# Reordering the weight splits of the pair jobs in a hybrid encoder layer, and two small products from high and low parts

## The chip, the cores and the metric

The kernel runs on one core of a Trainium2 chip. The time is that of one execution on the device, in microseconds (us). Shown are the median and the spread of several runs, and one execution taken by the hardware profiler. The engines are TensorE (PE, with its weight loads PEld), VectorE (DVE), ScalarE (ACT), GpSimd (POOL) and SyncE (SP, which issues DMAs). Each takes its instructions in the order in which the program lists them.

## The reference

One layer of a streaming encoder for 512 tokens of width 1024, all in float32: a SwiGLU feed-forward network (FFN, hidden width 2816) with half a residual, a mixer (a gated linear recurrence beside sliding-window attention), and a second FFN. Each is wrapped in RMS norms. What bears on the change is cut to this:

```python
def swiglu(x, w1, w3, w2):
    return (jax.nn.silu(x @ w1) * (x @ w3)) @ w2

f = swiglu(rms_norm(h, ffn1_pre_g), ffn1_w1, ffn1_w3, ffn1_w2)
h = h + 0.5 * rms_norm(f, ffn1_post_g)
...                      # mixer; attention adds bias = table[buckets]
f = swiglu(rms_norm(h, ffn2_pre_g), ffn2_w1, ffn2_w3, ffn2_w2)
h = h + 0.5 * rms_norm(f, ffn2_post_g)
```

## The kernel before, in words

Products must be accurate to float32, and the fast float32r format keeps fewer bits. So every operand is split: `split2` lets ScalarE copy it into float32r (the high part, `hi`) and VectorE subtract that copy from the original (the low part, `lo`). Each product is then three: high by high, low weight by high, high weight by low.

The up-projections w1 and w3 of both FFNs run mostly as *pair jobs* (class `Pairs`). A job takes two blocks of 128 hidden units of one of the two weights and computes their outputs for all 512 tokens as a 2x2 block product, by a Strassen scheme of the Winograd form: seven block products instead of eight, paid with sums of blocks. The blocks of the weight are a11, a12 (first raw tile, `ra`) and a21, a22 (second, `rb`). The weight sums are S1 = a21 + a22, S2 = S1 - a11 (one tile, `S12`), S3 = a11 - a21, S4 = a12 - S2 (one tile, `S34`). The activations' sums T1 to T4 are made once. A block product (`mm_s`, L464) is 12 products of 256 columns: 4 slices of the contraction, each the three of high and low parts.

The first FFN has 18 jobs (w1 and w3 in turn, job 0 to 17), the second 20. In `run` a job's products stand in this order: a11, S1, then a22 of the job before (it adds to a bank that the job before still holds, `last`, L591), S2, a12, S4, S3. Between them the next job is prepared, by `prep(m, i)`: i = 0 makes S1 and S2 (on GpSimd from job 2 on, and two jobs ahead), i = 1 splits `ra`, i = 2 makes S3 and S4 on VectorE and splits `S12`, i = 3 splits `S34`, i = 4 splits a22. ScalarE also copies four banks of each job to SBUF: q1 (L550), q5 (L553), u (L559) and v (L579). The bank of v is the one to which the next job's a22 product adds, so that product waits for the copy of v. In the first FFN the input norm's factor per token (`Rb`) is multiplied in behind the product: after an odd job's a22 product ScalarE copies the bank (L594), VectorE multiplies the w1 output with `Rb` (L595), and ScalarE takes the silu of it (L596), which `run` issues behind the next split of S34.

In the last job, a12 comes last, and `tail` (`w2_ahead`) splits two hidden units and two weights for the down-projection ahead of time.

Two small products are made in full float32, which TensorE takes in several passes: the row factor (`factor`, L714: ones times four diagonal matrices, so that each token's factor stands in all partitions), and the bias rows (`bias_rows`, L730: the relative-bias table times a one-hot matrix, 16 by 384), which stands between a11 and S1 of job 3.

Tiles of up to 4 KB per partition come from a pool of 42 slots; a tile that is given back is taken by a later one, which then waits for the last reader. The tiles `gap` and `gap2` hold nothing: they only shift the addresses of what follows.

Of the kernel before, what the change touches and what calls it, by code (L numbers as in the profile page):

```python
# [51 lines left out]
def hybrid_layer(ctx: ExitStack, tc: tile.TileContext, a: dict, out: bass.AP):  # L52
# [10 lines left out]
    def slot(shape, dt=F32, name="s"):  # L63
        uid[0] += 1
        return sb.tile(shape, dt, tag="slot", name=f"{name}_{uid[0]}")
# [5 lines left out]
    def small(w, name="m", bufs=4):  # L71
        uid[0] += 1
        return sm.tile([P, w], F32, tag=f"sm{w}", name=f"{name}_{uid[0]}", bufs={1: 11, 4: 12}.get(w, bufs))
# [11 lines left out]

    veps = cp.tile([P, NT], F32, name="veps")

    cp.tile([P, 172], F32, name="gap")
    sm.tile([P, 256], F32, name="gap2", bufs=1)
    uT = cp.tile([P, 2, KT, SEQ], F32R, name="uT")  # L90


# [383 lines left out]
    class Pairs:  # L476
# [14 lines left out]
        def prep(self, m, i, eng=None):  # L491
            if m >= len(self.jobs) or (m, i) in self.ready:
                return
            self.ready.add((m, i))
            k = self.k0 + 2 * m
            if i == 0:
                if k not in loaded or k + 1 not in loaded:
                    self.raws(m)
                s12, s34 = slot([P, 2 * QH], name="S12"), slot([P, 2 * QH], name="S34")
                self.w[m] = {"r": (raws.pop(k), raws.pop(k + 1)), "s": (s12, s34)}  # L500
            W = self.w[m]
            (ra, rb), (s12, s34) = W["r"], W["s"]
            a11, a12, a21, a22 = ra[:, :QH], ra[:, QH:], rb[:, :QH], rb[:, QH:]

            def both(src, w=2 * QH):
                hi = slot([P, w], F32R, name="whi")
                lo = slot([P, w], F32R, name="wlo")
                split2(hi, lo, src)
                return hi, lo

            def halves(p, a, b):
                W[a] = p[0][:, :QH], p[1][:, :QH]
                W[b] = p[0][:, QH:], p[1][:, QH:]

            if i == 0:
                e = eng or pool
                e.tensor_tensor(out=s12[:, :QH], in0=a21, in1=a22, op=ALU.add)
                e.tensor_tensor(out=s12[:, QH:], in0=s12[:, :QH], in1=a11, op=ALU.subtract)
            elif i == 1:
                halves(both(ra), "a11", "a12")  # L520
            elif i == 2:
                dve.tensor_tensor(out=s34[:, QH:], in0=a12, in1=s12[:, QH:], op=ALU.subtract)
                dve.tensor_tensor(out=s34[:, :QH], in0=a11, in1=a21, op=ALU.subtract)  # L523
                halves(both(s12), "s1", "s2")
            elif i == 3:
                halves(both(s34), "s3", "s4")
            elif i == 4:
                t = slot([P, 2, QH], F32R, name="w22")
                split2(t[:, 0, :], t[:, 1, :], a22)
                W["a22"] = t[:, 0, :], t[:, 1, :]  # L530
            if all((m, x) in self.ready for x in range(5)):
                del W["r"], W["s"]

        def run(self, tail, hooks={}):
            X = self.X
            assert st["get"] == st["split"] == self.k0, (st, self.k0)
            st["get"] = st["split"] = self.k0 + 2 * len(self.jobs)
            last = silu = lambda: None
            for n, (nm, f) in enumerate(self.jobs):
                W = self.w.pop(n)  # L540
                first = nm == self.na
                tmp = slot([P, 4, 256], name="ct")
                q1, q5, u, v = (tmp[:, i, :] for i in range(4))
                c = slot([P, 2, SEQ], name="cc")
                if first:
                    self.c1[f] = c
                bu, bx, bc = (bank("c")[:, :256] for _ in range(3))
                at = lambda i: [f() for f in hooks.get((n, i), ())]
                mm_s(W["a11"], X["b11"], bu)
                act.activation(q1, bu, AF.Copy)  # L550
                at(1)
                mm_s(W["s1"], X["t1"], bx)
                act.activation(q5, bx, AF.Copy)  # L553
                at(2)
                silu = last() or silu
                self.prep(n + 1, 1)
                mm_s(W["s2"], X["t2"], bu, True)
                del W["s1"], W["s2"]
                act.activation(u, bu, AF.Copy)  # L559
                at(3)  # L560
                if n == len(self.jobs) - 1:
                    tail()
                self.prep(n + 1, 2)

                def c11():
                    mm_s(W["a12"], X["b21"], bc)
                    del W["a11"], W["a12"]
                    dve.tensor_tensor(out=c[:, 0, :256], in0=bc, in1=q1, op=ALU.add)

                if n < len(self.jobs) - 1:  # L570
                    c11()
                mm_s(W["s4"], X["b22"], bx, True)
                dve.tensor_tensor(out=c[:, 0, 256:], in0=bx, in1=u, op=ALU.add)
                self.prep(n + 1, 3)
                silu()
                silu = lambda: None
                mm_s(W["s3"], X["t3"], bu, True)
                del W["s3"], W["s4"]
                act.activation(v, bu, AF.Copy)  # L579
                dve.tensor_tensor(out=c[:, 1, 256:], in0=v, in1=q5, op=ALU.add)  # L580
                if n == len(self.jobs) - 1:
                    c11()
                if not first:
                    c1 = self.c1[f]
                    dve.tensor_tensor(out=c1[:, 0, :], in0=c1[:, 0, :], in1=c[:, 0, :], op=ALU.mult)
                    dve.tensor_tensor(out=c1[:, 1, 256:], in0=c1[:, 1, 256:], in1=c[:, 1, 256:], op=ALU.mult)
                self.prep(n + 1, 4)
                self.prep(n + 2, 0)
                self.raws(n + 3)

                def last(W=W, bu=bu, c=c, f=f, first=first):  # L591
                    mm_s(W.pop("a22"), X["t4"], bu, True)
                    if first and self.R is not None:
                        act.activation(c[:, 1, :256], bu, AF.Copy)  # L594
                        dve.tensor_tensor(out=c, in0=c, in1=self.R, op=ALU.mult)  # L595
                        return lambda: act.activation(c, c, AF.Silu)  # L596
                    if first:
                        act.activation(c[:, 1, :256], bu, AF.Silu)
                        act.activation(c[:, 0, :], c[:, 0, :], AF.Silu)
                        act.activation(c[:, 1, 256:], c[:, 1, 256:], AF.Silu)  # L600
                    else:
                        c1 = self.c1.pop(f)
                        dve.tensor_tensor(out=c1[:, 1, :256], in0=bu, in1=c1[:, 1, :256], op=ALU.mult)
                        self.hid.f += [c1[:, 0, :], c1[:, 1, :]]

            last()
# [47 lines left out]
    dma_one(pairs_a.k0)  # L654
    dma_one(pairs_a.k0 + 1)
    make_identity(nc, ident)
    ones = slot([P, P], name="ones")
    pool.memset(ones, 1.0)
    ps = [bank("f") for _ in range(NS)]

    def split_first(u, kp):
# [34 lines left out]
    def t_split(n):  # L696
        X1[f"t{n + 1}"] = to_slots(tg[n])

    dgs = slot([P, NT, P], name="dgs")

    s4 = small(NT, "s4")

    def squares():
        for t in range(NT):
# [3 lines left out]
    def root():  # L708
        r = rstd4(s4)
        act.activation(tiny, tiny, AF.Silu)  # L710
        for t in range(NT):
            dve.tensor_scalar(out=dgs[:, t, :], in0=ident, scalar1=r[:, t : t + 1], scalar2=NEWT, op0=ALU.mult, op1=ALU.mult)

    def factor():  # L714
        psr = bank("r")
        for t in range(NT):
            pe.matmul(psr[:, t * P : (t + 1) * P], ones, dgs[:, t, :], start=True, stop=True)
        for i in range(2):
            act.activation(Rb[:, i, :], psr, AF.Copy)

# [2 lines left out]
    oh, erow = [], []  # L723

    def bias_in():
        oh.append(slot([N_BUCKETS, NREL + 1 + N_HEADS], name="oh"))
        pool.dma_start(out=oh[0][:, : NREL + 1], in_=a["onehot"])
        pool.dma_start(out=oh[0][:, NREL + 1 :], in_=a["rel_bias"])

    def bias_rows():  # L730
        pse = bank("e")
        t = oh.pop()
        pe.matmul(pse[:N_HEADS, : NREL + 1], t[:, NREL + 1 :], t[:, : NREL + 1], start=True, stop=True)
        erow.append(slot([N_HEADS, NREL + 1], name="erow"))
        act.activation(erow[0], pse[:N_HEADS, : NREL + 1], AF.Copy)

# [88 lines left out]
        late[4 + i, 1] = [lambda i=i: bias_spread(i)]  # L825

    def w2_ahead():
        hid.to(1)
        split_to(st["split"] + 1)
        hid.to(2)  # L830
        split_to(st["split"] + 1)

    pairs_a.run(w2_ahead, late)
# [460 lines left out]
```

## Time and profile before

| What | Value |
|---|---|
| Median of 3 runs | 1136.23 us (1135.98 to 1136.77) |
| The profiled execution: its time, and its span | 1137.54 us, 1135.5 us |
| TensorE busy | 1125.4 us (99%) |
| VectorE busy | 790.0 us (70%) |
| ScalarE busy | 597.8 us (53%) |
| GpSimd busy | 241.1 us (21%) |
| Pair jobs of the first FFN | from 50.9 to about 236 us |
| Pair jobs of the second FFN | from 806.4 to about 1008 us |
| Granted TensorE clock | 0.998 |

The profile gives for each instruction the engine, its line in the kernel, the tiles that it writes and reads, its start and its duration. A record of a product overlaps the next, so TensorE's busy time says little about its pace; the distance between the starts of products says it. Idle time before an instruction is given with what ended it, and a line such as L194 is that of a helper (`split2`): the tiles tell who called it.

### The profile page before, as it was taken

The numbers are of one execution on the slowest core, as the hardware profiler recorded it, in microseconds if no ns is written. First come the engines' busy times: TensorE is split into PE (matmuls) and PEld (weight loads), VectorE is DVE, ScalarE is ACT, GpSimd is POOL, SyncE is SP. The second block draws the span as 40 slices with busy tenths as digits, with TensorE's granted clock in tenths as the row PEclk, the third lists the DMA queues.
The fourth block names the chain that finished last, engine by engine and source line by source line (L and its number), as shares of the span: only waits on it lengthen the run. The fifth ranks groups of instructions, "written<-read, shape, count | busy, mean of one in ns | idle before, by whom it ended". The sixth has DMA issues, their size and how long they took to land.

```text
span 1135.5 us, 17456 instructions
## 1 busy us (share of the span) xinstructions
PE 1125.4 (99%) x6835; PEld 1006.0 (89%) x6835; DVE 790.0 (70%) x1252; ACT 597.8 (53%) x1060; POOL 241.1 (21%) x203
## 2 busy tenths in 40 slices
PE   9999999999999999999999999999999999999997
PEld 7899999988888987888888888889999999998886
DVE  5898989885336747695678865767787777885313
ACT  7755655574324349944656653356555555573211
POOL 0035444200000000001555641000533233300000
PEclk9999999999999999999999999999999999999999
DMA  9235563264313411234122333531333332265101
GB/s 324 96 103 137 122 150 113 75 222 151 110 56 130 149 57 56 75 94 148 56 80 89 93 102 103 187 109 39 111 101 99 100 112 94 74 195 176 38 19 56
DMA packets 37139, 124.95 MB, mean 110 GB/s; under 512 B 4529, under 2 KB 6449, under 8 KB 37057
## 3 DMA queue, kind: packets, MB, share of 16 engines
q1 hardware_dynamic: 34272, 115.15, 30.8%
q0 software_dynamic: 2640, 8.43, 3.8%
q8 instruction: 53, 0.87, 0.3%
q10 hardware_dynamic: 144, 0.26, 0.1%
q14 instruction: 30, 0.24, 0.1%
HBM read 116.50 MB, written 7.33 MB: 109 GB/s over the span
## 4 chain that ended last, share of the span: by engine, by line
PE 91%; DVE 5%; ACT 3%; issue 1%; DMA 0%; SPq 0%; DVEq 0%; ACTq 0%
PE c L472 10%; PE f L203 10%; PE f L204 10%; PE f L205 10%; PE c L473 10%; PE c L471 10%; PE acc L222 8%; PE acc L223 8%; PE acc L221 8%; DVE wlo L194 2%; PE pt L1097 1%; PE s L1061 1%; PE s L1060 1%; DVE S L523 1%; PE tr L313 1%
## 5 line engine op out<-in xcount | busy, mean ns | idle before, releaser
L203 PE MATMUL f<-uT,whi 128*128 128x512 f32 (+1 forms) x472 | 171.7, 364 | 0.0
L204 PE MATMUL f<-uT,wlo 128*128 128x512 f32 (+1 forms) x472 | 170.4, 361 | 0.1
L205 PE MATMUL f<-uT,whi 128*128 128x512 f32 (+1 forms) x472 | 170.1, 360 | 0.0
L221 PE MATMUL acc<-whi,hT 128*128 128x512 f32 x352 | 137.1, 390 | 0.0
L222 PE MATMUL acc<-wlo,hT 128*128 128x512 f32 x352 | 137.0, 389 | 0.0
L223 PE MATMUL acc<-whi,hT 128*128 128x512 f32 x352 | 136.9, 389 | 0.0
L472 PE MATMUL c<-Xh,wlo 128*128 128x256 f32 x456 | 129.8, 285 | 1.1 <-DVE wlo L194 0.6
L471 PE MATMUL c<-Xh,whi 128*128 128x256 f32 x456 | 129.1, 283 | 0.0
L472 PE MATMUL c<-uT,wlo 128*128 128x256 f32 x456 | 129.0, 283 | 0.0
L471 PE MATMUL c<-uT,whi 128*128 128x256 f32 x456 | 129.0, 283 | 0.0
L473 PE MATMUL c<-uT,whi 128*128 128x256 f32 x456 | 129.0, 283 | 0.0
L473 PE MATMUL c<-Xl,whi 128*128 128x256 f32 x456 | 129.0, 283 | 0.0
L193 ACT ACTIVATE whi<-S 128x1024 fp32r<-128x1024 f32 x76 | 80.2, 1057 | 53.0 <-DVE S L523 53.0
L194 DVE TENSOR_TENSOR wlo<-S,whi 128x1024 fp32r<-128x1024 f32 x76 | 101.9, 1341 | 0.3 <-ACT whi L193 0.3
L203 PEld LDWEIGHTS f<-uT,whi 128*128 128x128 f32 x472 | 89.1, 189 | 14.5 <-issue 1.4
L204 PEld LDWEIGHTS f<-uT,wlo 128*128 128x128 f32 x472 | 89.2, 189 | 13.8 <-DVE wlo L159 0.9
L205 PEld LDWEIGHTS f<-uT,whi 128*128 128x128 f32 x472 | 89.1, 189 | 13.5
L472 PEld LDWEIGHTS c<-Xh,wlo 128*128 128x128 f32 x456 | 87.5, 192 | 2.4 <-DVE wlo L194 2.4
L471 PEld LDWEIGHTS c<-Xh,whi 128*128 128x128 f32 x456 | 87.5, 192 | 0.6 <-ACT ct L550 0.6
L471 PEld LDWEIGHTS c<-uT,whi 128*128 128x128 f32 x456 | 87.5, 192 | 0.0
L472 PEld LDWEIGHTS c<-uT,wlo 128*128 128x128 f32 x456 | 87.5, 192 | 0.0
L473 PEld LDWEIGHTS c<-uT,whi 128*128 128x128 f32 x456 | 87.5, 192 | 0.0
(312 smaller groups left out, 2646.8 us busy)
## 6 DMA issues: line engine op xcount, KB each, us to landing
raw_w2a<-in_w2a_dram SPq DMA_DIRECT2D x22, 512.0 KB, 4.4
raw_w1b<-in_w1b_dram SPq DMA_DIRECT2D x22, 512.0 KB, 3.9
raw_w3b<-in_w3b_dram SPq DMA_DIRECT2D x22, 512.0 KB, 4.0
raw_w2b<-in_w2b_dram SPq DMA_DIRECT2D x22, 512.0 KB, 4.4
raw_w3a<-in_w3a_dram SPq DMA_DIRECT2D x21, 512.0 KB, 4.5
raw_w1a<-in_w1a_dram SPq DMA_DIRECT2D x20, 512.0 KB, 4.3
raw_wg<-in_wg_dram SPq DMA_DIRECT2D x16, 512.0 KB, 4.0
raw_xr<-in_xr_dram SPq DMA_DIRECT2D x8, 512.0 KB, 4.0
```

The costliest lines, as they stand in the source:

```text
L193: act.activation(hi, src, AF.Copy)
L194: dve.tensor_tensor(out=lo, in0=src, in1=f32(hi), op=ALU.subtract)
L203: pe.matmul(ps[:, c0:c1], wh[:, s], h_, start=k == 0, stop=False)
L204: pe.matmul(ps[:, c0:c1], wl[:, s], h_, start=False, stop=False)
L205: pe.matmul(ps[:, c0:c1], wh[:, s], l_, start=False, stop=k == KT - 1)
L221: pe.matmul(acc[n], x[:, 0, c], wh[:, s], start=first, stop=False)
L222: pe.matmul(acc[n], x[:, 0, c], wl[:, s], start=False, stop=False)
L223: pe.matmul(acc[n], x[:, 1, c], wh[:, s], start=False, stop=last)
L313: pe.transpose(ps[:, k * P : (k + 1) * P], hg[:, kk * P : (kk + 1) * P], ident)
L471: pe.matmul(ps, wh[:, s], xh, start=first, stop=False, skip_group_check=True)
L472: pe.matmul(ps, wl[:, s], xh, start=False, stop=False, skip_group_check=True)
L473: pe.matmul(ps, wh[:, s], xl, start=False, stop=k == 3, skip_group_check=True)
```

## The change

Six edits:

- `prep(n + 1, 1)`, the split of the next job's first raw tile, is issued before the work of the former job's a22 product, not behind it.
- In `prep(m, 2)` the split of S1 and S2 is issued before VectorE's sums S4 and S3.
- In the last job the silu comes first, directly behind the copy of u. `tail` now splits one hidden unit and one weight, and is called twice: behind the silu, and behind the copy of v.
- The row factor is made from high and low parts: the factor is rounded to float32r (`rh`), the rest is the low part (`rl`), each makes four diagonals on VectorE (eight where there were four), and TensorE multiplies ones with all four diagonals at once, in two products of 512 columns that add up.
- The bias rows are made from the table's high and low part: ScalarE copies one-hot matrix and table into float32r, VectorE makes the low part, and TensorE adds up two products.
- `gap` shrinks from 172 to 168 floats and `gap2` from 256 to 240; two small tiles are new. In the built program `uT` and all slots lie 32 bytes lower than before, the slots at multiples of 4096 bytes.

The order of the instructions on GpSimd and SyncE is the same in both programs.

```diff
             elif i == 2:
+                halves(both(s12), "s1", "s2")
                 dve.tensor_tensor(out=s34[:, QH:], in0=a12, in1=s12[:, QH:], op=ALU.subtract)
                 dve.tensor_tensor(out=s34[:, :QH], in0=a11, in1=a21, op=ALU.subtract)
-                halves(both(s12), "s1", "s2")
...
                 at(2)
+                self.prep(n + 1, 1)
                 silu = last() or silu
-                self.prep(n + 1, 1)
                 mm_s(W["s2"], X["t2"], bu, True)
                 del W["s1"], W["s2"]
                 act.activation(u, bu, AF.Copy)
                 at(3)
                 if n == len(self.jobs) - 1:
+                    silu()
+                    silu = lambda: None
                     tail()
...
                 if n == len(self.jobs) - 1:
+                    tail()
                     c11()
...
-    dgs = slot([P, NT, P], name="dgs")
+    dgs = [slot([P, NT, P], F32R, name="dgs") for _ in range(2)]
+    tiny_r = [sm.tile([P, NT], F32R, tag="smr", name=f"rn{n}", bufs=2) for n in range(2)]
...
-        for t in range(NT):
-            dve.tensor_scalar(out=dgs[:, t, :], in0=ident, scalar1=r[:, t : t + 1], scalar2=NEWT, op0=ALU.mult, op1=ALU.mult)
+        rh, rl = tiny_r
+        dve.tensor_scalar(out=rh, in0=r, scalar1=NEWT, scalar2=None, op0=ALU.mult)
+        dve.scalar_tensor_tensor(out=rl, in0=r, scalar=NEWT, in1=f32(rh), op0=ALU.mult, op1=ALU.subtract)
+        for x, d_ in zip(tiny_r, dgs):
+            for t in range(NT):
+                dve.tensor_scalar(out=d_[:, t, :], in0=ident, scalar1=f32(x)[:, t : t + 1], scalar2=None, op0=ALU.mult)
...
-        for t in range(NT):
-            pe.matmul(psr[:, t * P : (t + 1) * P], ones, dgs[:, t, :], start=True, stop=True)
+        for n, d_ in enumerate(dgs):
+            pe.matmul(psr, ones, d_.rearrange("p t q -> p (t q)"), start=n == 0, stop=n == 1)
...
-        t = oh.pop()
-        pe.matmul(pse[:N_HEADS, : NREL + 1], t[:, NREL + 1 :], t[:, : NREL + 1], start=True, stop=True)
+        t, u = oh
+        oh.clear()
+        n = NREL + 1
+        hi, lo = u[:, n : n + N_HEADS], u[:, n + N_HEADS :]
+        act.activation(u[:, : n + N_HEADS], t, AF.Copy)
+        dve.tensor_tensor(out=lo, in0=t[:, n:], in1=f32(hi), op=ALU.subtract)
+        pe.matmul(pse[:N_HEADS, :n], hi, u[:, :n], start=True, stop=False)
+        pe.matmul(pse[:N_HEADS, :n], lo, u[:, :n], start=False, stop=True)
...
     def w2_ahead():
-        hid.to(1)
-        split_to(st["split"] + 1)
-        hid.to(2)
+        hid.to(hid.done + 1)
         split_to(st["split"] + 1)
```

More of the change, by code (lines that the diff above doesn't have):

```diff
@@ L86, in hybrid_layer @@
     veps = cp.tile([P, NT], F32, name="veps")
-    cp.tile([P, 172], F32, name="gap")
-    sm.tile([P, 256], F32, name="gap2", bufs=1)
+    cp.tile([P, 168], F32, name="gap")
+    sm.tile([P, 240], F32, name="gap2", bufs=1)
     uT = cp.tile([P, 2, KT, SEQ], F32R, name="uT")
@@ L656, in hybrid_layer @@
     make_identity(nc, ident)
-    ones = slot([P, P], name="ones")
-    pool.memset(ones, 1.0)
+    ones = slot([P, P], F32R, name="ones")
+    pool.memset(f32(ones), 1.0)
     ps = [bank("f") for _ in range(NS)]
@@ L725, in bias_in @@
     def bias_in():
-        oh.append(slot([N_BUCKETS, NREL + 1 + N_HEADS], name="oh"))
+        oh.extend((slot([N_BUCKETS, NREL + 1 + N_HEADS], name="oh"), slot([N_BUCKETS, NREL + 1 + 2 * N_HEADS], F32R, name="ohr")))
         pool.dma_start(out=oh[0][:, : NREL + 1], in_=a["onehot"])
```

## The prediction

> **What bounds the kernel now.** I read the page's busy table and chain first, then the timeline of each engine around every place where the products' starts stand apart.
>
> ```profile
> PE 1125.4 (99%) x6835; PEld 1006.0 (89%) x6835; DVE 790.0 (70%) x1252; ACT 597.8 (53%) x1060; POOL 241.1 (21%) x203
> PE 91%; DVE 5%; ACT 3%; issue 1%; DMA 0%; SPq 0%; DVEq 0%; ACTq 0%
> ```
>
> TensorE is the bound (99% busy, 91% of the chain), and the change takes next to no product away. So it can win only what TensorE waits, and busy time hides that, because a product's record overlaps the next. The starts show it. This is the timeline of TensorE in the pair jobs (start, duration, line, output and inputs):
>
> ```profile
> 61.06 0.28 PE L471 MATMUL c<-Xh,whi 128*128 128x256 f32 x1
> 61.93 0.39 PE L472 MATMUL c<-Xh,wlo 128*128 128x256 f32 x1 [0.59 <-DVE wlo L194]
> 62.15 0.28 PE L473 MATMUL c<-Xl,whi 128*128 128x256 f32 x1
> ...
> 93.12 0.28 PE L471 MATMUL c<-Xh,whi 128*128 128x256 f32 x1
> 93.49 0.39 PE L472 MATMUL c<-Xh,wlo 128*128 128x256 f32 x1
> 93.72 0.28 PE L473 MATMUL c<-Xl,whi 128*128 128x256 f32 x1
> ...
> 154.65 0.28 PE L471 MATMUL c<-Xh,whi 128*128 128x256 f32 x1
> 155.02 0.38 PE L472 MATMUL c<-Xh,wlo 128*128 128x256 f32 x1
> ...
> 234.07 0.28 PE L473 MATMUL c<-uT,whi 128*128 128x256 f32 x1
> 234.66 0.39 PE L471 MATMUL c<-Xh,w 128*128 128x256 f32 x1 [0.31 <-ACT ct L579]
> ...
> 967.71 0.28 PE L471 MATMUL c<-Xh,whi 128*128 128x256 f32 x1
> 967.95 0.39 PE L472 MATMUL c<-Xh,wlo 128*128 128x256 f32 x1
> ...
> 988.09 0.28 PE L471 MATMUL c<-Xh,whi 128*128 128x256 f32 x1
> 988.45 0.39 PE L472 MATMUL c<-Xh,wlo 128*128 128x256 f32 x1
> ```
>
> Undisturbed, products of 256 columns start 0.12 us apart (62.15 is late by the 0.10 that follows each wait: 0.22 from 61.93). Seven times the first product with the low part of S1 comes late. At 61.06 it loses 0.87 - 0.12 + 0.10 = 0.85; at 93.12 0.37 - 0.12 + 0.11 = 0.36, and so four times (jobs 4, 6, 8, 10 of the first FFN; first and last shown), 1.43; at 967.71 0.22 and at 988.09 0.34. Sum 2.84 us. At 234.07, in the last job of the first FFN, the product with a22 waits for the copy of S3's bank (v, L579): 0.59 - 0.12 + 0.10 = 0.57. All of it together is 3.4 us, 0.3% of the span: that is the most the reordering can give.
>
> **S1 and S2 split first, the first weight split sooner.** I follow job 3, which prepares job 4, on VectorE, ScalarE and GpSimd:
>
> ```profile
> 86.53 1.23 DVE L595 TENSOR_TENSOR cc<-cc,Rb 128x1024 f32<-128x1024 f32 x1 [2.46 <-ACT cc L594]
> 87.67 2.33 DVE L194 TENSOR_TENSOR wlo<-raw_w1a,whi 128x1024 fp32r<-128x1024 f32 x1
> 89.92 1.78 DVE L522 TENSOR_TENSOR S<-raw_w1a,S 128x512 f32<-128x512 f32 x1
> 91.63 0.68 DVE L523 TENSOR_TENSOR S<-raw_w1a,raw_w1a 128x512 f32<-128x512 f32 x1
> ...
> 99.71 1.21 DVE L194 TENSOR_TENSOR wlo<-S,whi 128x1024 fp32r<-128x1024 f32 x1
> ```
> ```profile
> 84.68 0.38 ACT L553 ACTIVATE ct<-c 128x256 f32<-128x256 f32 x1 [1.09 <-PE c L473]
> 87.84 1.05 ACT L193 ACTIVATE whi<-S 128x1024 fp32r<-128x1024 f32 x1
> 92.40 1.06 ACT L193 ACTIVATE whi<-S 128x1024 fp32r<-128x1024 f32 x1 [3.51 <-DVE S L523]
> 93.36 1.04 ACT L596 ACTIVATE cc<-cc 128x1024 f32<-128x1024 f32 x1
> 94.31 0.36 ACT L579 ACTIVATE ct<-c 128x256 f32<-128x256 f32 x1
> ```
> ```profile
> 87.48 1.44 POOL L517 TENSOR_TENSOR S<-raw_w3a 128x512 f32<-128x512 f32 x1 [8.43 <-PE c L472]
> ...
> 97.91 4.17 POOL L517 TENSOR_TENSOR S<-raw_w1a 128x512 f32<-128x512 f32 x1 [6.23 <-PE c L472]
> ```
>
> Now VectorE stands idle 2.46 us behind L595 while the first weight could be split. In the changed order ScalarE copies its high part right after L553 (from 84.96 to 86.01), VectorE splits it by 87.14, L595 runs to 88.28, and the split of S1 and S2 waits only for its own high part (87.84 + 1.05 = 88.89). It ends at 90.1 alone, or 92.3 when GpSimd gets in twice; its reader is due at 93.24. So the 2.84 us of S1 waits go: I take all of it in the first FFN.
>
> But the sums S3 and S4 now come after that split: alone they end at 88.92 + 1.13 + 0.60 + 0.68 = 91.3 (pitches are the durations less the 0.08 by which records overlap). ScalarE's in-order queue has the high part of S3, S4 (waits for the sums, 3.51 us even now), then the silu L596, then the copy L579, which must be done before the product with a22 may write that bank, and that product is due 12 x 0.12 = 1.44 after 93.12, at 94.56. By the rows L579 ends 2.36 after the sums (92.31 to 94.67). With nothing in the way it ends at 93.7, 0.9 early. What is late next is therefore this copy. GpSimd's two sums for the job after next decide: 87.67 took 2.33 against 1.21 at 99.71, so each GpSimd sum that goes first costs a VectorE instruction 1.1. One such block puts L579's end at 94.8 and makes the product wait 0.35 (with 0.10 behind it); two blocks 1.45; none, as at 97.91, where the GpSimd instruction itself took 4.17 while VectorE went on at 1.21, costs nothing. In jobs 3 and 5 GpSimd is issued (87.48) before VectorE's split can be (88.92) and finds only L595's end in its way, so one sum has 0.6 alone: I take one block, 0.35 each for jobs 4 and 6. In jobs 7 and 9 VectorE's split is ready first by a hair:
>
> ```profile
> 149.37 1.05 ACT L193 ACTIVATE whi<-S 128x1024 fp32r<-128x1024 f32 x1
> ...
> 150.58 1.60 POOL L517 TENSOR_TENSOR S<-raw_w3a 128x512 f32<-128x512 f32 x1 [4.74 <-PE c L473]
> ```
>
> (150.42 against 150.58.) One block would cost 0.27, two 1.4; I take 0.27 in one of the two. Jobs 4 to 10: 0.97 for 1.43, -0.46; bounds -1.43 and 2 x 1.45 + 2 x 1.4 - 1.43 = +4.3. In the second FFN no such silu stands before the copy and the reader is due later than the copy by more, so of 0.56 I take -0.40 (bounds -0.56 and 0).
>
> The Trainium skill, page "SBUF — State Buffer", section "Who interferes with whom", says that a VectorE instruction with two SBUF inputs and a reading GpSimd instruction exclude one another, and that whoever issues first holds the port pair for its whole instruction. The row at 87.67 agrees, the one at 97.91 too. Taken strictly it speaks against this change in jobs 3 and 5: GpSimd issues first there, which is the slow rival below.
>
> **Silu first in the last job.** L579 follows two hidden-unit splits, two weight splits and the silu on ScalarE; the change puts the silu and one pair ahead and the other behind. The copy can then follow its product at once: -0.57. The moved weight split is needed only by the next stage's second round, so I cost it at nothing; if that cover went, it would be one copy of 1.05.
>
> **The two small products.** The row factor, four full fp32 products of 128 columns (8 records), and the bias rows (2 records):
>
> ```profile
> 36.02 0.88 DVE L712 TENSOR_SCALAR dgs<-ident,r 128x128 f32<-128x128 f32 x4
> ...
> 38.98 0.39 PE L205 MATMUL f<-uT,whi 128*128 128x512 f32 x1
> 39.20 1.05 PE L717 MATMUL r<-dgs,ones 128*128 128x128 f32 x8
> 40.01 0.48 PE L203 MATMUL f<-uT,whi 128*128 128x512 f32 x1
> ...
> 82.19 0.81 PE L733 MATMUL e<-oh 32*16 32x384 f32 x2
> 82.94 0.39 PE L471 MATMUL c<-Xh,whi 128*128 128x256 f32 x1
> ```
> ```profile
> 82.30 0.38 ACT L550 ACTIVATE ct<-c 128x256 f32<-128x256 f32 x1
> 83.10 0.48 ACT L735 ACTIVATE erow<-e 16x384 f32<-16x384 f32 x1 [0.42 <-PE e L733]
> ```
> ```profile
> 83.40 0.68 DVE L194 TENSOR_TENSOR w<-raw_w3a,w 128x512 fp32r<-128x512 f32 x1
> ```
> ```profile
> 55.50:84.10 28.60, 28.01 (x227) 27.04 (x226) 28.38 (x33) 15.37 (x26) 11.35 (x8) 1.00 0.34 116
> ```
>
> The factor goes from 0.81 (39.20 to 40.01) to two products of 512 columns at 0.22 each: -0.4. Four more diagonals (0.88) and two tiny instructions end near 38.1, before 39.20: hidden. The bias product is different. It stood ready before; now its operands are made on the spot. ScalarE copies 32x400 (nearest row 0.48) behind L550, so to 83.06, and TensorE, which has nothing else in order, stands until then. Then VectorE must make the low part, and it is in order behind the split at 83.40. The last row (a stretch: length, then busy time of PE, PEld, DVE, ACT, POOL) says that VectorE is busy 28.38 of 28.60 us up to there: it has no slack, the change takes no work from it and only reorders, so it reaches the low part at about 84.1 as before, whatever TensorE has gained. The second product can start near 84.2 and S1 near 84.35, against 82.94: TensorE is +1.4 at that point, and the gains of the factor (0.4) and of job 1 (0.85) lie inside that. Bounds: if reordering lets VectorE run free of GpSimd, ScalarE's copy alone is the floor (S1 at a11's end + 1.5 instead of + 0.85), -0.4 - 0.85 + 0.65 = -0.6; with 1.1 more of blocking, +2.5. SP's and GpSimd's own order of instructions stays as it was.
>
> All slots and uT also move down by 32 bytes. No row prices that: products on uT and on slots both start 0.12 apart. I take 0, though 1 ns on each of 6835 records would be 6.8 us.
>
> **Sum.** +1.4 (to job 3) - 0.46 (jobs 4 to 10) - 0.57 (last job) - 0.40 (second FFN) = 0.0 us. The profiled execution took 1137.54 (span 1135.5), 1.3 above the median of 1136.23; against the median the forecast is **1136.2 us**. 0.2% of it, 2.3 us, is about what a measurement of this kernel can tell from no change.
>
> **Rivals.** *Waits go and none comes* (faster): VectorE keeps the port with back-to-back splits, GpSimd waits as at 97.91, L579 keeps its 0.9, VectorE reaches the low part early. -0.6 - 1.43 - 0.57 - 0.56 = -3.2: 1133.0 us. For it: 97.91; against: 87.48, 28.38 of 28.60. Chance 0.25.
> *GpSimd goes first* (slower): both its sums fall on S1's split and on the sums, S3's high part holds L579 back, the product with a22 waits in jobs 4 to 10. +1.4 + 4.3 - 0.57 - 0.40 = +4.7: 1140.9 us. It decides from sums that end less than 2.36 before a22's product is due, that is after 92.2. For it: 87.48 precedes 88.92; against: GpSimd has L595's gap to itself. Chance 0.2.
> *The change does not do what it says*: S1's high part would have to wait for GpSimd, but that sum is made over 7 us ahead (87.48 for the copy of the next job), so I give this no chance of its own.
> My forecast has 0.55. Range 1133.0 to 1139.7, between the fast rival and three quarters of the slow one.
>
> **What would show it.** Right: in the changed profile no product waits for wlo at S1; waits appear at the product with a22 with L581 (the copy, two lines lower) as releaser; 1.2 to 1.7 us more between a11's end and S1 in job 3; the last job's 0.57 gone. Wrong: the bias product within 0.5 us of a11's end, a22 waits over 1 us in several jobs, or another start spacing than 0.12 everywhere.

## The result, and the profile after

The changed kernel takes 1142.84 us (median of 6 runs, 1142.35 to 1142.97), the kernel before 1136.11: a ratio of 1.0057, with a 95% interval from 1.0044 to 1.0070. It is slower by 6.7 us, where 1136.2 was forecast. The profiled execution took 1142.35 us, its span 1140.6, which is 5.1 over the span before (1135.5). The one of before lay 1.4 above its own median, so the medians stand further apart than the spans.

The busy times and the chain of the changed kernel, from the page:

```profile
PE 1124.6 (99%) x6829; PEld 1006.0 (88%) x6829; DVE 798.3 (70%) x1259; ACT 593.7 (52%) x1061; POOL 228.6 (20%) x203
PE 87%; DVE 6%; ACT 5%; issue 2%; DMA 0%; DVEq 0%; ACTq 0%
```

TensorE is as busy as before, and its share of the chain has fallen from 91% to 87%: ScalarE and VectorE have taken more of the path. Where they do so is seen in the starts of the products (the timeline of TensorE in the changed kernel: start, duration, line, output and inputs, idle time and its releaser):

```profile
61.33 0.28 PE L473 MATMUL c<-Xl,whi 128*128 128x256 f32 x1
62.10 0.39 PE L471 MATMUL c<-Xh,w 128*128 128x256 f32 x1 [0.50 <-ACT ct L581]
...
72.15 0.28 PE L473 MATMUL c<-Xl,whi 128*128 128x256 f32 x1
73.25 0.39 PE L471 MATMUL c<-Xh,w 128*128 128x256 f32 x1 [0.82 <-ACT ct L581]
...
81.86 0.28 PE L473 MATMUL c<-uT,whi 128*128 128x256 f32 x1
83.55 0.34 PE L746 MATMUL e<-ohr 32*16 32x384 f32 x1 [1.41 <-ACT ohr L744]
84.34 0.34 PE L747 MATMUL e<-ohr 32*16 32x384 f32 x1 [0.46 <-DVE ohr L745]
84.61 0.39 PE L471 MATMUL c<-Xh,whi 128*128 128x256 f32 x1
...
96.11 0.28 PE L473 MATMUL c<-Xl,whi 128*128 128x256 f32 x1
97.03 0.39 PE L471 MATMUL c<-Xh,w 128*128 128x256 f32 x1 [0.64 <-ACT ct L581]
...
138.22 0.28 PE L473 MATMUL c<-Xl,whi 128*128 128x256 f32 x1
139.69 0.39 PE L471 MATMUL c<-Xh,w 128*128 128x256 f32 x1 [1.20 <-ACT ct L581]
...
149.75 0.28 PE L473 MATMUL c<-Xl,whi 128*128 128x256 f32 x1
150.28 0.39 PE L471 MATMUL c<-Xh,w 128*128 128x256 f32 x1 [0.25 <-ACT ct L581]
...
240.55 0.28 PE L473 MATMUL c<-uT,whi 128*128 128x256 f32 x1
240.67 0.28 PE L471 MATMUL c<-Xh,w 128*128 128x256 f32 x1
```

No product waits for the low part of S1 any more, and the last job's product with a22 starts 0.12 after the one ahead of it. In their place the first product with a22 waits for the copy of v (now L581) in nine jobs, and each such wait is the distance less 0.12 and plus the 0.10 that follows: 0.75 in job 1, 1.08 in job 2, 0.90 each in jobs 4 and 6 (97.03 shown), 1.45 each in jobs 8 and 10 (139.69), and 0.51 each in jobs 9, 11 and 13 (150.28). That is 8.1 us. Between the last product of a11 and S1 in job 3 lie 2.75 us (81.86 to 84.61), where the old form of the bias product had 0.96.

How the copy comes late is seen in jobs 7 and 3. ScalarE in job 7 of the changed kernel:

```profile
131.62 1.05 ACT L193 ACTIVATE whi<-S 128x1024 fp32r<-128x1024 f32 x1
137.37 1.06 ACT L193 ACTIVATE whi<-S 128x1024 fp32r<-128x1024 f32 x1 [4.70 <-DVE S L524]
138.33 1.04 ACT L599 ACTIVATE cc<-cc 128x1024 f32<-128x1024 f32 x1
139.28 0.36 ACT L581 ACTIVATE ct<-c 128x256 f32<-128x256 f32 x1
```

VectorE in job 3 (first three rows) and in job 7, and GpSimd in job 7:

```profile
90.59 1.72 DVE L194 TENSOR_TENSOR wlo<-S,whi 128x1024 fp32r<-128x1024 f32 x1 [0.52 <-ACT whi L193]
92.23 1.77 DVE L523 TENSOR_TENSOR S<-raw_w1a,S 128x512 f32<-128x512 f32 x1
93.93 0.68 DVE L524 TENSOR_TENSOR S<-raw_w1a,raw_w1a 128x512 f32<-128x512 f32 x1
...
132.70 1.23 DVE L194 TENSOR_TENSOR wlo<-S,whi 128x1024 fp32r<-128x1024 f32 x1 [0.52 <-ACT whi L193]
133.84 1.78 DVE L523 TENSOR_TENSOR S<-raw_w1a,S 128x512 f32<-128x512 f32 x1
135.55 1.78 DVE L524 TENSOR_TENSOR S<-raw_w1a,raw_w1a 128x512 f32<-128x512 f32 x1
```
```profile
132.71 2.37 POOL L517 TENSOR_TENSOR S<-raw_w3a 128x512 f32<-128x512 f32 x1 [7.20 <-PE c L472]
135.16 1.62 POOL L518 TENSOR_TENSOR S<-S,raw_w3a 128x512 f32<-128x512 f32 x1
```

ScalarE stands 4.70 us for the sums, then does the high part of S3 and S4 and the silu, and only then the copy that TensorE needs at 138.34. GpSimd starts its two sums just when VectorE starts the split of S1 and S2, and each of VectorE's two sums behind it then takes 1.78 in place of 0.68: two blocks of 1.1. In job 3 the split (1.72 for 1.22) and one sum (1.77) share 1.6 us.

### The profile page after: what moved, and what is told of

It reads as the page before. It is cut to its first block, busy times and chain, and to the rows that moved or that the text cites. A ratio compares the mean times of both kernels' runs of the same rounds, so it can differ in the third digit from the quotient of the medians.

```text
span 1140.6 us, 17421 instructions
## 1 busy us (share of the span) xinstructions
PE 1124.6 (99%) x6829; PEld 1006.0 (88%) x6829; DVE 798.3 (70%) x1259; ACT 593.7 (52%) x1061; POOL 228.6 (20%) x203
## 4 chain that ended last, share of the span: by engine, by line
PE 87%; DVE 6%; ACT 5%; issue 2%; DMA 0%; DVEq 0%; ACTq 0%
PE f L203 10%; PE f L204 10%; PE f L205 10%; PE c L471 9%; PE c L473 9%; PE c L472 9%; PE acc L221 8%; PE acc L222 8%; PE acc L223 8%; ACT whi L193 2%; DVE wlo L194 1%; DVE S L523 1%; PE pt L1109 1%; DVE S L524 1%; PE s L1073 1%
## 5 line engine op out<-in xcount | busy, mean ns | idle before, releaser
L471 PEld LDWEIGHTS c<-uT,whi 128*128 128x128 f32 x456 | 87.7, 192 | 0.0
L473 PEld LDWEIGHTS c<-Xl,whi 128*128 128x128 f32 x456 | 87.7, 192 | 0.0
```

Source lines behind the costliest of these rows:

```text
L471: pe.matmul(ps, wh[:, s], xh, start=first, stop=False, skip_group_check=True)
L473: pe.matmul(ps, wh[:, s], xl, start=False, stop=k == 3, skip_group_check=True)
```

## The experiments

Three theories were set against each other: the *queue theory* (the copy of v is late because ScalarE, in order, has the high part of S3 and S4 ahead of it), the *port theory* (GpSimd holds VectorE back, whatever stands in the order), and the *small-products theory* (the bias product and the addresses carry the loss).

**v first.** The changed kernel with the copy of v moved ahead in ScalarE's order:

```diff
-                self.prep(n + 1, 3)
-                silu()
-                silu = lambda: None
                 mm_s(W["s3"], X["t3"], bu, True)
                 act.activation(v, bu, AF.Copy)
                 dve.tensor_tensor(out=c[:, 1, 256:], in0=v, in1=q5, op=ALU.add)
+                self.prep(n + 1, 3)
+                silu()
+                silu = lambda: None
```

> The changed kernel with one move: the copy of S3's bank (v) is issued ahead of the high part of S3 and S4 and of the silu on ScalarE. Queue theory: the nine waits of the product with a22 in jobs 1 to 13 (8.1 us with what follows each) exist only because v stands in ScalarE's order behind that high part, which waits for the two sums on VectorE; moved ahead, all nine go and no other product becomes late, since S3 and S4 are wanted only a job later: 1142.8 - 8.1 = 1134.7 us, 1134 to 1136. Port theory: the time comes from VectorE's sums being held by GpSimd's sums, whatever stands in ScalarE's order; the lateness then only moves to the products with S4 or S3, and the time stays above 1140. Small-products theory: the 6.7 us lie in the bias and factor products and in the moved addresses, and the time stays within 1 us of 1142.8.

Measured: 1138.3 us, ratio to before 1.0015 (1.0006 to 1.0024). All nine waits for v are gone, so the order is their cause; but 3.6 us of the expected gain came back. ScalarE, then TensorE in this run, and a stretch of 4 us (its length; busy time and count of PE, PEld, DVE, ACT and POOL; granted clock, DMA share, GB/s):

```profile
134.81 0.38 ACT L578 ACTIVATE ct<-c 128x256 f32<-128x256 f32 x1 [2.99 <-PE c L473]
136.52 1.06 ACT L193 ACTIVATE whi<-S 128x1024 fp32r<-128x1024 f32 x1 [1.32 <-DVE S L524]
137.49 1.04 ACT L599 ACTIVATE cc<-cc 128x1024 f32<-128x1024 f32 x1
138.43 0.61 ACT L193 ACTIVATE w<-raw_w1a 128x512 fp32r<-128x512 f32 x1
138.96 0.36 ACT L550 ACTIVATE ct<-c 128x256 f32<-128x256 f32 x1
```
```profile
138.81 0.28 PE L473 MATMUL c<-Xl,w 128*128 128x256 f32 x1
139.37 0.38 PE L471 MATMUL c<-Xh,whi 128*128 128x256 f32 x1 [0.27 <-ACT ct L550]
```
```profile
84.00:88.00 4.00, 4.00 (x21) 3.93 (x21) 0.00 (x0) 1.73 (x3) 0.00 (x0) 0.57 0.01 4
```

v is now copied at 134.81, in good time. But the same late queue stands ahead of the next copy, q1 (L550), and the product with S2 adds to that bank: it waits at 72.95, 138.81 and 159.50 (0.57, 0.43 and 0.44, with 0.1 each behind, 1.7 us in all). The bias product waits 2.1 instead of 1.6. The rest is the clock: right behind that wait it was granted at 0.57 for 4 us, and TensorE's products start 0.21 apart from 84.4 to 87.8, which costs 1.5 us. Together that is 3.7.

**The order of the sums, both ways.** The changed kernel with the sums first again, and the kernel before with the split first alone (the same edit, backwards):

```diff
             elif i == 2:
-                halves(both(s12), "s1", "s2")
                 dve.tensor_tensor(out=s34[:, QH:], in0=a12, in1=s12[:, QH:], op=ALU.subtract)
                 dve.tensor_tensor(out=s34[:, :QH], in0=a11, in1=a21, op=ALU.subtract)
+                halves(both(s12), "s1", "s2")
```

> The changed kernel with the sums S4 and S3 again ahead of the split of S1 and S2, all else as changed. Queue theory: the high part of S3 and S4 no longer waits for late sums, so the a22 waits go (8.1 us); the product with the low part of S1 has its 0.36 us waits back at most in four jobs, less since the first weight is still split sooner: 1134.7 to 1136.2 us. Port theory: the sums meet GpSimd elsewhere and hold the same ScalarE queue: 1138 to 1142. Small-products theory: within 1 us of 1142.8.

> The kernel before with one part of the change alone: S1 and S2 split ahead of the sums S4 and S3. Queue theory: the S1 waits go (1.43 us) and the a22 waits come (jobs 1 to 13, 8.1 us or more, since the first weight is split later here and all behind it is later): 1136.1 + 6.7 = 1142.8, 1141 to 1145 us. Port theory: the same sign, 1139 to 1143. Small-products theory: no more than 1 us from 1136.1.

Measured: 1135.63 us (0.9996, 0.9987 to 1.0005) and 1144.32 us (1.0070, 1.0057 to 1.0082). This one edit makes the slowdown, alone and within the change. With the sums first, neither the a22 waits nor the S1 waits are there: all that is left in the first FFN's pair jobs is the bias product's.

**The first weight sooner, alone** (the kernel before with these two lines exchanged):

```diff
-                silu = last() or silu
                 self.prep(n + 1, 1)
+                silu = last() or silu
```

> The kernel before with one part alone: the next job's first weight split ahead of the copies of the a22 product. If this alone sets the time of the low part of S1, its waits in jobs 1, 4, 6, 8 and 10 shrink or go (0.85 + 1.43 us) and nothing else becomes late, since the sums stay ahead: 1136.3 - 1.4 to 2.3 = 1134.0 to 1134.9 us. If the split of S1 and S2 had to come ahead of the sums for that, 1136.0 to 1136.5.

Measured: 1134.12 us, 0.9980 (0.9971 to 0.9989). The S1 waits of jobs 4, 6, 8 and 10 and of the second FFN are gone, with nothing in their place; job 1's stays (0.82), and so does the last job's 0.57. So this one part gives nearly all the gain that the new order of the sums was meant to give.

**GpSimd's sums taken to VectorE**, in the first FFN of the changed kernel:

```diff
-                e = eng or pool
+                e = eng or (dve if self.R is not None else pool)
```

> The changed kernel with the two sums for S1 and S2 in the first feed-forward pair jobs on VectorE instead of GpSimd (0.68 us each there), all else as changed. If the wait chain needs GpSimd's blocks of 1.1 us under VectorE's sums, the sums S4 and S3 take 0.68 us in place of 1.78, the high part of S3 and S4 comes some 2 us sooner, and the a22 waits of jobs 4 to 13 go (0.90 + 0.90 + 1.46 + 1.46 + three of 0.51 = 6.2 us): 1136.6 us, 1136 to 1139, more where VectorE's 1.4 us more work in each job make something else late. If the place in ScalarE's order alone makes them: 1141 to 1143.

Measured: 1146.07 us, 1.0091 (1.0077 to 1.0105), outside what either side of the expectation gave. VectorE in this run, at one place and in an ordinary job:

```profile
117.58 0.69 DVE L517 TENSOR_TENSOR S<-raw_w1a 128x512 f32<-128x512 f32 x1 [10.72 <-DMA raw_w1a<-in_w1a_dram]
...
131.82 0.68 DVE L523 TENSOR_TENSOR S<-raw_w3a,S 128x512 f32<-128x512 f32 x1
132.42 0.68 DVE L524 TENSOR_TENSOR S<-raw_w3a,raw_w3a 128x512 f32<-128x512 f32 x1
```

The waits themselves do what was expected: without GpSimd the sums take 0.68 each, and the a22 waits are gone in all jobs but one. That one stands behind a stall of its own: VectorE, in order, stood 10.72 us for a weight that had not landed. TensorE lost 9.3 us there between 112 and 127: 7.3 in waits, and 2.0 because its products started 0.21 apart for a while (granted clock 0.50 from 120 to 124). Behind the bias product, which waits longer here, the clock was at 0.57 for 4 us as in the run with v first. In the changed kernel, with these sums on GpSimd, TensorE has no such stall. A second form issued the sums a job later:

```diff
                 at(2)
+                if self.R is not None:
+                    self.prep(n + 1, 0, dve)
                 self.prep(n + 1, 1)
...
-                self.prep(n + 2, 0)
+                if self.R is None:
+                    self.prep(n + 2, 0)
```

> The changed kernel with the two sums for S1 and S2 on VectorE again, now issued one job later, ahead of the first weight's split, so that VectorE's queue does not stand for a weight that has not landed (10.7 us in the run with them a job earlier). If GpSimd's blocks make the a22 waits: the sums S4 and S3 take 0.68 us each instead of 1.78, the sums for S1 and S2 take 1.4 us more, so the copy v comes about 0.85 us sooner in jobs 4 to 13; the waits of 0.90 shrink to about 0.05, those of 1.46 to 0.6, those of 0.51 go: 6.2 becomes 1.3, and jobs 1 and 2 gain up to 1.8: 1136 to 1138 us. If only the place in ScalarE's order matters: 1142 or more, for the queue is 1.4 us later.

Measured: 1141.06 us, 1.0047 (1.0035 to 1.0059). Again no a22 wait is left but one, at 119.12, and that lies behind the same stall, now 8.29 us of VectorE's and 3.65 of TensorE's, with a clock of 0.84 and 0.73 in the two stretches of 4 us from 112 on. So both are needed for the waits: the place in ScalarE's order, and GpSimd's blocks that make the sums late.

**The bias product.** The changed kernel with its old form, and the kernel with the sums first and the operands made in job 2 (the edit of the second, cut):

```diff
     def bias_rows():
-        act.activation(u[:, : n + N_HEADS], t, AF.Copy)
-        dve.tensor_tensor(out=lo, in0=t[:, n:], in1=f32(hi), op=ALU.subtract)
...
-    (3, 1): [bias_rows]
+    (2, 3): [bias_parts], (3, 1): [bias_rows]     # bias_parts: the two lines above
```

> The changed kernel with the bias product as before (one product of full float32 inputs, no rounding on ScalarE, no difference on VectorE). The trace of the changed kernel has 1.56 us of standing at that product, of which the old form had about a tenth: queue theory and port theory both give 1142.8 - 1.4 = 1141.4 us, 1140.8 to 1142.3; small-products theory, in which the products carry the loss, gives 1139 or less.

> The changed kernel with the sums S4 and S3 ahead of the split of S1 and S2 again, and with the two halves of the bias operands made in job 2 instead of right at the bias product in job 3. The kernel with the sums first took 1135.6 us and stood 1.05 us at the bias product and nowhere else in the first feed-forward pair jobs. If that wait is the late operands alone: 1135.6 - 1.05 = 1134.6 us, 1133.8 to 1135.3, below both kernels. If the rounding on ScalarE in job 2 makes that job's copies late instead, the wait moves there: 1135.4 to 1136.5.

Measured: 1140.67 us (1.0037, 1.0025 to 1.0050), 2.2 below the changed kernel, so most of the loss is not in this product; and 1133.08 us (0.9972, 0.9961 to 0.9982), below both kernels.

**S3 and S4 split behind q1.** v first, the silu behind it, `prep(n, 3)` moved to the next job's line behind the copy of q1; once with the bias operands made early, once not:

> The changed kernel with v copied first, the silu after it, the split of S3 and S4 moved behind the first copy of the next job (q1), and the bias operands made in job 2. With v first alone (1138.3 us) the product with S2 stood behind q1 (0.57, 0.43, 0.44 us and 0.1 after each) and the bias product 2.1 us. Queue theory: with S3 and S4 split behind q1 nothing on TensorE's way stands behind the sums: 1138.3 - 1.7 - 2.1 = 1134.5 us, 1133.8 to 1135.5. If the lateness only moves one place further (to q5's copy or the products with S4), 1136 to 1139.

> The kernel of 1132.7 us (v first, S3 and S4 split behind q1) with the bias operands made at the bias product again, as in the changed kernel. If the wait at the bias product is the rounding on ScalarE (0.5 us) and the difference behind VectorE's queue, it comes back with 1.0 to 2.1 us: 1133.7 to 1134.8. If it was the late queue of the changed kernel that made it long, it is 0.5 us or less: 1132.7 to 1133.2.

Measured: 1132.68 us (0.9968, 0.9956 to 0.9981) and 1136.78 us (0.9997, 0.9989 to 1.0006). With both, nothing on TensorE's way stands behind the sums, and no wait of over 0.1 us is left in the pair jobs, with the split of S1 and S2 still first. TensorE at the bias product in the first of the two:

```profile
80.19 0.28 PE L473 MATMUL c<-uT,whi 128*128 128x256 f32 x1
80.40 0.34 PE L752 MATMUL e<-ohr 32*16 32x384 f32 x1
80.59 0.33 PE L753 MATMUL e<-ohr 32*16 32x384 f32 x1
80.84 0.39 PE L471 MATMUL c<-Xh,whi 128*128 128x256 f32 x1
```

0.65 us in all, less than the 0.96 of the full float32 form; made on the spot it is 2.75 (changed kernel). With the second run, in which the operands are late again, the same stretch is 3.30 (80.17 to 83.47), 2.65 more. The profiled execution of the second (1135.38 us) lies 2.7 above the first kernel, as its trace says, but the median lies 4.1 above it. The other 1.4 go with the clock: in the four executions of 1135.4 to 1136.0 us its mean was 0.998 or 0.999, in the seven of 1136.7 to 1136.9 us it was 0.997.

**The small products alone**, on the kernel before:

> The kernel before with the two small products alone from high and low parts. The prediction's step: 0.4 us less at the factor, and the first product with S1 of job 3 late until VectorE reaches the low part of the bias operand, 1.4 us later than before in all, whatever was gained ahead of it: 1136.4 + 1.4 = 1137.8 us, 1137.2 to 1138.2. If the loss of the changed kernel lay in these products: 1140 or more. If VectorE has room there: 1136 to 1136.6.

Measured: 1134.37 us, 0.9979 (0.9970 to 0.9987): faster, which no theory had. The bias product waits as expected in its trace, but TensorE's products keep another pace. The two new small tiles lie ahead of the slots and move all of them by 64 bytes, which the change itself takes back with its shorter `gap2`. These edits separate the two:

```diff
 before + small products:  -    sm.tile([P, 256], F32, name="gap2", bufs=1)
                           +    sm.tile([P, 240], F32, name="gap2", bufs=1)
 before, nothing else:     -    sm.tile([P, 256], F32, name="gap2", bufs=1)
                           +    sm.tile([P, 272], F32, name="gap2", bufs=1)
 the 1132.7 us kernel:     -    sm.tile([P, 240], F32, name="gap2", bufs=1)
                           +    sm.tile([P, 256], F32, name="gap2", bufs=1)      (64 bytes; 248 for 32 bytes)
```

> The kernel before with the two small products alone, the second gap cut so that all slots keep their addresses. If the 2.1 us gained by the run of the small products came from the slots' addresses: starts 0.120 and 0.227 us apart again, and what is left is the products' own price, -0.4 at the factor and, by the runs with the bias operands made late, 2.5 us from the last product ahead of the bias product to S1 where the old form takes 0.95: +1.6, together 1136.4 + 1.2 = 1137.6 us, 1137.0 to 1138.3. If the products themselves gained: 1134.4 again.

> The kernel before with one edit: the second gap is 64 bytes longer, so that every slot lies 64 bytes further from uT; no instruction is added, removed or moved. Address theory: the pair jobs' products with uT start 0.114 to 0.115 us apart in place of 0.120 (some 1400 of them, -8 us), those of 512 columns with uT 0.233 in place of 0.227 (some 900, +5.5 us), and the S1 waits grow a little, since only TensorE is faster: 1136.4 - 3 = 1133.4 us, 1132.4 to 1134.4. If addresses do nothing: 1136.0 to 1136.8.

> The kernel of 1132.7 us (v first, S3 and S4 split behind q1, bias operands made in job 2) with the slots 64 bytes further from uT. Address theory, if it goes by the distance between slots and uT: the same spacings as above and -3 us, 1129.7 us, 1128.7 to 1131, as long as the other engines keep up with jobs that are some 3% shorter; if they don't, waits come back and it stays near 1132. If the absolute address counts, the spacing stays at 0.120 and the time at 1132.7.

> The same kernel with the slots 32 bytes further from uT. If any distance that is no multiple of 128 bytes gives the other spacing: 1129 to 1131 us as with 64. If only 64 does: 1132.7. A third spacing would give a time of its own, from 1129 to 1136.

Measured: the small products with the slots in their old places 1138.65 us (1.0015, 1.0006 to 1.0024); the kernel before with the slots 64 bytes further and no other difference 1131.75 us (0.9957, 0.9944 to 0.9970); the best version 1127.54 us with 64 bytes (0.9919, 0.9906 to 0.9932) and 1134.60 us with 32 (0.9983, 0.9974 to 0.9992). So the products by themselves cost 2.0 us by the medians, and the addresses are worth 4.9 to 5.1. Of the 2.0 the trace shows 1.2 (2.50 for 0.96 at the bias product, 0.45 for 0.81 at the factor); its execution took 1137.56 us at a mean clock of 0.999, while the six that lie at or above the median had 0.996 to 0.998. One stretch of the second FFN's pair jobs (60 us: busy time and count of PE, PEld, DVE, ACT, POOL, then clock, DMA share and GB/s), and two rows six products of 512 columns apart, in the kernel before:

```profile
890.00:950.00 60.00, 60.00 (x502) 60.00 (x502) 45.29 (x63) 32.79 (x58) 18.27 (x12) 1.00 0.32 106
```
```profile
389.94 0.39 PE L203 MATMUL f<-uT,whi 128*128 128x512 f32 x1
...
391.30 0.39 PE L203 MATMUL f<-uT,whi 128*128 128x512 f32 x1
```

and the same of the kernel before with only the slots moved:

```profile
890.00:950.00 60.00, 60.00 (x519) 60.00 (x518) 47.99 (x64) 33.37 (x58) 19.57 (x13) 1.00 0.32 102
```
```profile
389.81 0.39 PE L203 MATMUL f<-uT,whi 128*128 128x512 f32 x1
...
391.21 0.39 PE L203 MATMUL f<-uT,whi 128*128 128x512 f32 x1
```

There are 519 products in place of 502 in the same time, at the same clock: 0.1156 us each for 0.1195. Products of 512 columns with uT go the other way, 1.40 / 6 = 0.233 for 1.36 / 6 = 0.227. In the fastest version the chain of waits reads

```profile
PE 99%; DVE 0%; issue 0%; DVEq 0%; ACT 0%
```

## Why the prediction was wrong

By its own steps:

- **S1 waits go: right.** All seven are gone; the second FFN gave 0.56, where 0.40 was taken. But the first weight split sooner does this alone in all but job 1.
- **The factor: right.** 0.81 became 0.45 (38.60 to 39.05): 0.36 less, for 0.4.
- **The bias product: the size nearly right, the reason not.** S1 of job 3 starts at 84.61, against 82.94: +1.67 for +1.4. The step took VectorE to have no slack up to there, so that the time of the low part is fixed whatever TensorE gains. In the changed kernel VectorE did reach the low part at 84.14, but with the small products alone at 82.71, and S1 starts at 83.19: the time was not fixed. VectorE had begun that stretch 0.7 us sooner (54.83 for 55.50), and what counts as busy contains the time for which GpSimd holds it up, 1.6 us in job 0 there and 2.2 in the kernel before (its split of S1 and S2 at 59.55 took 2.33). So 28.38 of 28.60 is not all work. By parts the +1.67 is 2.75 - 0.96 = 1.79 for the bias product itself, +1.83 for the a22 waits of jobs 1 and 2, which the step did not have, -0.85 for job 1's S1 wait, and -1.06 for pair jobs that begin sooner (49.93 for 50.99: 0.36 of it is the factor, the rest lies in the first stage, whose waits differ between executions): 1.71.
- **Last job's silu first: right.** Its 0.57 is gone in every run that has this edit, and there in those that lack it (the first weight sooner alone, the split first alone).
- **The shift by 32 bytes: right, by luck.** uT and the slots moved together, and the pace stayed at 0.120 and 0.227. That moving one against the other is worth 4.9 us was not seen; no row of one profile shows it.
- **The copy of v: the step that failed.** The place, the order and the price were right: a copy that is late by the blocks that fall on the sums, 0.90 for 1.6 us of them in jobs 4 and 6, where the text has 0.35 for one block of 1.1 and 1.45 for two, and 1.45 for 2.2 in jobs 8 and 10, where it has 1.4 for two. Wrong was their number. It took one block of 1.1 in jobs 3 and 5, and one in one of jobs 7 and 9, since VectorE's split would start first there "by a hair". VectorE's split did start first (132.70 against 132.71) and ran free, but both of the sums behind it were held: GpSimd had two instructions pending, and VectorE lost time to both, 2.2 us in job 7. In job 3 it lost 1.6. And the jobs without a silu were left out: 9, 11 and 13 wait 0.51 each. So jobs 4 to 13 stand at 0.90 + 0.90 + 1.45 + 1.45 + 1.53 - 1.43 = +4.8 where -0.46 was written, above even the +4.3 that the text gave as the bound. These 5.3 us are most of the 6.6 by which the forecast was short. The 1.83 of jobs 1 and 2 were not in this step either; they stand in the +1.67 up to job 3. The rest lies between executions: the profiled one of before was 1.4 over its median, that of the changed kernel 0.5 under.

The sum over the trace: +1.67 + 4.8 - 0.57 - 0.56 = +5.3, against 5.1 between the spans. The rival "GpSimd goes first" (1140.9 us, chance 0.2) came nearest: GpSimd's sums held VectorE up and the copy of v came late in jobs 4 to 10, though in job 7 GpSimd did not go first. It stopped short by the jobs without a silu. The rule of the Trainium skill, page "SBUF — State Buffer", section "Who interferes with whom", which was cited for it (the two engines exclude one another for a whole instruction), agrees with the runs: 0.68 us for a sum without GpSimd beside it, 1.78 with it. It does not say who goes next when both have more pending, and that decided here: at 97.91 in the kernel before VectorE went on while GpSimd stood, in job 7 of the changed kernel the two took turns.

## What to carry to other kernels

Moving work ahead on one engine moves the rest behind, and the cost shows where an in-order queue couples things that have nothing to do with one another: here a copy that frees a PSUM bank stood behind a cast that waits for sums on VectorE. List, for each engine, what stands behind the first instruction that waits, and put what TensorE needs next ahead of it; that, with the bias operands made sooner, was worth 10 us between two orders of the same work (1142.8 and 1132.7). Where a wait rests on two engines that hold each other up, take as the bound a block (1.1 us here) for every instruction that finds the other engine with work pending, in every job, not only in those that have waits now. When an edit adds a tile, check what it does to the addresses before its time is read. And compare the granted clock of the executions before a difference of 1 or 2 us is explained by the program.

## What was not expected of the hardware

- The pace of TensorE's products depends on how far the slots, in which the weights lie, are from uT, which streams. In the kernel before, and in the changed one, where slots and uT both lie 32 bytes lower, products of 256 columns start 0.120 us apart and those of 512 columns 0.227. With the slots 64 bytes further away it is 0.1145 on average for products of 256 columns with uT in the pair jobs, and 0.233 for 512; with 32 bytes about 0.118 and 0.233. In that last kernel the slots lie where the kernel before has them and uT where the changed one has it, so neither address alone sets the pace. Since the two kinds of product prefer different distances, a layout that gave each stage its own might be worth more; that was not tried, and why the distance matters stays open.
- The granted clock can fall for some us behind a wait of TensorE, to 0.50 by the rows (products of 256 columns 0.21 apart for 0.12), and that is worth 1 to 2 us in some executions and not in others of the same kernel. A mean under 0.998 is seen only in kernels in which the bias product waits, and not in the kernel before, in those with the old form of that product, or in those with its operands made early. In the changed kernel itself, which has that wait, all six executions had 0.999, so the clock has no part in its 6.7 us. What decides whether it falls was not tested.
